# One paced list for the modulation columns of a conditioned two-layer trunk, with loads three columns ahead

## The chip, the cores and the metric

The kernel runs on one core of a Trainium2 chip. The metric is the device time of one execution in microseconds; lower is better.

## The reference

A trunk of two layers over 512 tokens of width 1024 in float32. A conditioning vector `c` gives every layer its shifts, scales and gates:

```
cs  = silu(c)
mod = cs @ mod_w[l] + mod_b[l]         # 6 x 1024 values: sh1, sc1, gt1, sh2, sc2, gt2
h = rmsnorm(x)*g*(1 + sc1) + sh1
x = x + gt1 * mixer(h)                 # layer 0: gated DeltaNet with 8 heads, layer 1: differential attention
h = rmsnorm(x)*g*(1 + sc2) + sh2
x = x + gt2 * (relu(h @ w1)**2 @ w2)   # w1 1024 x 4096, w2 4096 x 1024
```

Layer 1 also reads a shared `kv` projection, modulated by `cs @ kv_mod_w`. A last rmsnorm ends it. In all 96 + 16 = 112 columns of 128 modulation values are computed, each from a 128 x 1024 block of weights.

## The kernel before

**Data.** Activations lie with the features on the partitions: `x` is eight tiles of 128 x 512 (features x tokens). Every large product is done in three matmuls (`three`, L275 to L278): weights and activations are split in a high and a low part, and high by high, high by low and low by high are summed. `weights` (L264) loads a pair of weight tiles (`raw`, three buffers, 512 KB mostly), copies the high part on ACT (`wh`, L269), and subtracts for the low part (`wl`, L260), on DVE for the heads, gates and `w_out`, on POOL for the MLP. It then calls `mod_next` (L272).

**Order of the stages in layer 0.** The program first norms and modulates `x`, using columns 0 to 15; those are loaded at once and do not change here. Then come eight heads: `proj_head` (projection) and the generator `gdn` (three parts: the triangular inverse, the scan over four chunks, the output), each head's later parts overlapping the next head's projection. The gate projections follow, then head 7's last part, then `close_block` for `a_w_out` (L728): the first half of its columns in one piece (`proj_T`, then `add_resid` at L334), the second half in two token halves of 256 (`proj_halves`), where `done` adds the residual (L322), norms (L236 to L242) and modulates (L252 to L255). The block opens the second set of PSUM banks only when the first `add_resid` has read the old ones. MLP 0 follows: four quarters of `w1` (q0 to q3), with `relu` and square at L744 to L749, then `w2` in two column pieces of 16 row tiles, each ended by `add_resid` from the same four `j` banks; then the same again for the second half of the hidden width.

**The modulation columns.** A column is one load of 128 x 1024 float32 (512 KB, L181, on SP's queue) into a tile `mw`, and one instruction on DVE (L182, "a dot") that multiplies by `cs` and sums into one column of `raw_mod`. `mod_bias` and `mod_gsc` then finish groups of eight. Columns 16 to 23 are issued after head 3 and 24 to 31 after head 5, eight at a time (L704 to L708). Columns 32 to 111 stand in a list; each call of `weights` adds `rate` to a counter and takes that many columns off (L185): 1 in `w_out`, 1.2 in MLP 0. `mw` has two buffers, so a load waits for the dot two columns earlier. In columns 32, 33, 40 and 41 a one-element copy on POOL (L180, `gate_on`) makes the load wait for the output of head 4, or for a modulated tile of MLP 0's input.

**What sets the order.** Each engine runs its instructions in one fixed order, and so does SP with its loads. That order is not the order of the code: a scheduler in the framework places each engine's instructions ahead of time, so an edit of the list moves instructions of other lines too. The rows of the two orders below are its result.

Of the kernel before, what the change touches and what calls it, by code (L numbers as in the profile page):

```python
# [10 lines left out]
F32 = mybir.dt.float32  # L11
# [19 lines left out]
RAW = 3  # L31
MB = 8
NE = (0, 1, 2, 1, 2, 0, 1, 0)
CV = 9
GH = 4
GX = 7

# [3 lines left out]
C_GMIX = C_KVMODB + 16  # L41
# [43 lines left out]
def trunk_kernel(ctx: ExitStack, tc: tile.TileContext, a, outT):  # L85
# [32 lines left out]
    def big(pool, tag, bufs, dt=F32):  # L118
        return pool.tile([P, S], dt, tag=tag, name=nm(tag), bufs=bufs)
# [53 lines left out]

    queue, rate, due, gate_on = [], [0], [0], {}

    def mod_col(c, after=None, pool=None, bufs=2):
        src = a["mod_wT"][c * P:(c + 1) * P, :] if c < 96 else a["kv_mod_wT"][(c - 96) * P:(c - 95) * P, :]
        w = (pool or c_pool).tile([P, D], F32, tag="mw", name=nm("mw"), bufs=bufs)
        if after is not None:
            G.tensor_copy(w[0:1, 0:1], after[0:1, 0:1])  # L180
        nc.sync.dma_start(w, src)  # L181
        V.scalar_tensor_tensor(out=w, in0=w, scalar=1.0, in1=cs, op0=ALU.mult, op1=ALU.mult,  # L182
                               accum_out=raw_mod[:, c:c + 1])

    def mod_next(n):  # L185

        due[0] += n
        while due[0] >= 1 and queue:
            due[0] -= 1
            c, then = queue.pop(0)  # L190
            mod_col(c, gate_on.pop(c, None))
            for f in then:
                f()

    def mod_bias(lo, hi):
        V.tensor_tensor(out=mod[:, lo:hi], in0=raw_mod[:, lo:hi], in1=cols[:, lo:hi], op=ALU.add)
# [183 lines left out]
    for k0 in range(0, KT, 2):  # L380
        ws = []
        for h in range(2):
            k = k0 + h
            mod_col(SH1 + k, None, m_pool, MB)
            mod_col(SC1 + k, None, m_pool, MB)
            both = slice(k, k + 9, 8)
            V.tensor_tensor(out=mod[:, both], in0=raw_mod[:, both], in1=cols[:, both], op=ALU.add)
            mod_gsc(k, SC1 + k, C_GMIX + k, 1)
            modulate(k, xs, rb, 0, SH1, hh, hl, FULL)
            ws.append(head_weights(h, k0))  # L390
# [93 lines left out]
    def gdn(h):  # L484
# [27 lines left out]
        pk = natural(kT[h])  # L512
        kn = big(g_pool, "kn", 4)
        A.activation(kn, pk, AF.Copy)
# [8 lines left out]

        bq = [big(g_pool, "bq", 8) for _ in range(2)]
        for n in range(2):
# [161 lines left out]
    def gate(h0, n):  # L687
        ps = proj_T(cols_of(w_in, 3072 + P * h0, P * n), KT, hh, hl, ntile=n)
        for j in range(n):
# [3 lines left out]
            if oT[h] is not None:  # L693
                V.tensor_tensor(out=oT[h], in0=sz[h], in1=oT[h], op=ALU.mult)

    heads = []
    for h in range(H):
        proj_head(h)
        heads.append(gdn(h))
        next(heads[h])  # L700
        next(heads[h])
        if h:
            next(heads[h - 1], None)
        if h in (3, 5):  # L704
            c0 = 16 if h == 3 else 24
            for c in range(c0, c0 + 8):
                mod_col(c)
            mod_bias(c0, c0 + 8)  # L708
    for i in range(0, H, 2):
        gate(i, 2)  # L710
    next(heads[H - 1], None)
    for c in range(32, 112):
        queue.append((c, []))
    for c, j, sc, g_ in ((40, 8, SC2, C_GMLP), (64, 16, 48 + SC1, C_GMIX + 8), (88, 24, 48 + SC2, C_GMLP + 8), (112, 32, 104, C_GKV)):
        queue[c - 33][1].append(lambda j=j, sc=sc, g_=g_: mod_gsc(j, sc, g_))
    for c in range(40, 113, 8):
        queue[c - 33][1].insert(0, lambda c=c: mod_bias(c - 8, c))
    rate[0] = 1
    gate_on.update({32: oT[GH], 33: oT[GH]})
    g_st.close()  # L720
# [47 lines left out]

    rate[0] = 1.2
    gate_on.update({c: uh[GX].bitcast(F32) for c in (40, 41)})  # L770
    mlp(0, uh, ul, after0)
# [219 lines left out]
```

## Time and profile before

| | |
|---|---|
| median of 3 runs | 1413.43 us (1410.11 to 1415.57) |
| profiled execution | 1411.8 us |
| its span in the trace | 1410.0 us |
| PE busy | 1313.9 us, 93% |
| DVE busy | 800.0 us, 57% |
| ACT, POOL busy | 510.0 us, 481.9 us |
| mean granted TensorE clock | 0.977 |

The span is what the trace covers; the profiled execution's own time is 1.8 us longer, and lies 1.6 us under the median. PE is busy nearly throughout, so a change of the time has to be read from the 96 us in which it is not, and from what may be added to them. A full-width matmul (128 x 512) begins every 0.227 us when PE does not wait; a pair of weight tiles for four output tiles is 24 of these, 5.45 us.

### The profile page before, as it was taken

What the parts mean: (1) busy time and instruction counts of PE and PEld (TensorE: products, weight loads), DVE (VectorE), ACT (ScalarE), POOL (GpSimd) and SP (SyncE); (2) the same over time, 40 slices, a digit from 0 to 9 for tenths busy, and PEclk for the clock granted to TensorE, in tenths of its full rate; (3) what the DMA queues carried; (4) which work ended last, traced back from release to release, by engine and by line L of the source; (5) the groups of instructions that cost most, each with busy time, mean ns of one, the idle gap of its engine ahead of it and who ended that gap; (6) DMA issues with size and microseconds to landing.
All of it is one profiled execution on the core that took longest, in us unless ns stands there. A gap on an engine that the chain in (4) does not pass through costs nothing. (4 is left out here: it accounts for less than half of the span.)

```text
span 1410.0 us, 19521 instructions
## 1 busy us (share of the span) xinstructions
PE 1313.9 (93%) x7432; PEld 1111.3 (79%) x7432; DVE 800.0 (57%) x1688; ACT 510.0 (36%) x853; POOL 481.9 (34%) x285
## 2 busy tenths in 40 slices
PE   4888799899999999499999999999999999999997
PEld 3666687777789887388888998888798888888896
DVE  6999889788767877657311377777652110021113
ACT  3384234442424332122432244444434331243321
POOL 3324213221105454244544213232234444444441
PEclk9999699999999999799999999999999999999999
DMA  9542162112555777776322233221122232223221
GB/s 313 182 116 59 31 174 64 50 34 67 166 185 180 264 228 254 253 256 237 118 92 96 82 104 100 80 64 65 60 76 105 90 105 90 105 90 105 91 75 60
DMA packets 113214, 174.99 MB, mean 124 GB/s; under 512 B 16384, under 2 KB 56992, under 8 KB 113120
## 3 DMA queue, kind: packets, MB, share of 16 engines
q1 hardware_dynamic: 112416, 172.92, 37.6%
q8 instruction: 58, 0.95, 0.3%
q10 hardware_dynamic: 704, 0.83, 0.2%
q14 instruction: 36, 0.29, 0.1%
HBM read 170.04 MB, written 2.62 MB: 122 GB/s over the span
## 5 line engine op out<-in xcount | busy, mean ns | idle before, releaser
L260 POOL TENSOR_TENSOR wl<-raw,wh 128x1024 fp32r<-128x1024 f32 (+1 forms) x137 | 340.7, 2491 | 407.4 <-ACT wh L269 401.8
L269 ACT ACTIVATE wh<-raw 128x1024 fp32r<-128x1024 f32 (+2 forms) x217 | 215.4, 996 | 495.4 <-PE pj L277 279.8
L276 PE MATMUL pj<-h,wh 128*128 128x512 f32 (+1 forms) x816 | 290.8, 360 | 19.1 <-ACT h L254 7.6
L278 PE MATMUL pj<-h,wl 128*128 128x512 f32 (+1 forms) x816 | 290.4, 358 | 0.0
L277 PE MATMUL pj<-h,wh 128*128 128x512 f32 (+1 forms) x816 | 289.8, 355 | 0.0
L182 DVE SCALAR_TENSOR_TENSOR mw<-mw,cs 128x1024 f32<-128x1024 f32 x112 | 181.8, 1626 | 67.8 <-DMA mw<-in_mod_wT_dram 54.1
L276 PE MATMUL pj<-u,wh 128*128 128x512 f32 (+1 forms) x512 | 172.9, 338 | 17.7 <-DVE x L322 17.7
L276 PEld LDWEIGHTS pj<-h,wh 128*128 128x128 f32 x816 | 155.9, 192 | 40.2 <-ACT h L254 10.1
L278 PE MATMUL pj<-u,wl 128*128 128x512 f32 (+1 forms) x512 | 173.1, 338 | 2.7 <-POOL wl L260 2.7
L277 PE MATMUL pj<-u,wh 128*128 128x512 f32 (+1 forms) x512 | 172.9, 338 | 0.0
L277 PEld LDWEIGHTS pj<-h,wh 128*128 128x128 f32 x816 | 156.3, 192 | 17.9 <-DVE h L255 0.3
L278 PEld LDWEIGHTS pj<-h,wl 128*128 128x128 f32 x816 | 156.2, 192 | 18.1
L276 PEld LDWEIGHTS pj<-u,wh 128*128 128x128 f32 x512 | 97.7, 191 | 28.2 <-issue 18.1
L322 DVE SCALAR_TENSOR_TENSOR x<-pj,mod,x 128x256 f32<-128x256 f32 (+1 forms) x53 | 30.2, 585 | 156.3 <-PE pj L278 156.3
L278 PEld LDWEIGHTS pj<-u,wl 128*128 128x128 f32 x512 | 97.6, 191 | 13.6 <-POOL wl L260 3.5
L277 PEld LDWEIGHTS pj<-u,wh 128*128 128x128 f32 x512 | 97.6, 191 | 10.3
L260 DVE TENSOR_TENSOR wl<-raw,wh 128x1024 fp32r<-128x1024 f32 (+2 forms) x80 | 85.4, 1069 | 18.8 <-ACT wh L269 18.3
L745 DVE SCALAR_TENSOR_TENSOR pj<-pj,r 128x512 f32<-128x512 f32 x32 | 21.8, 693 | 71.7 <-ACT r L744 71.5
L745 DVE SCALAR_TENSOR_TENSOR pn<-pn,r 128x512 f32<-128x512 f32 x16 | 11.1, 693 | 74.8 <-ACT r L744 74.8
L276 PE MATMUL pn<-h,wh 128*128 128x512 f32 x128 | 49.8, 389 | 0.0
L277 PE MATMUL pn<-h,wh 128*128 128x512 f32 x128 | 49.8, 389 | 0.0
L278 PE MATMUL pn<-h,wl 128*128 128x512 f32 x128 | 49.8, 389 | 0.0
(297 smaller groups left out, 2366.5 us busy)
## 6 DMA issues: line engine op xcount, KB each, us to landing
raw<-in_mlp_w_dram SPq DMA_DIRECT2D x128, 512.0 KB, 3.6
mw<-in_mod_wT_dram SPq DMA_DIRECT2D x96, 512.0 KB, 4.4
raw<-in_a_w_in_dram SPq DMA_DIRECT2D x96, 128.0 KB, 2.5
mw<-in_kv_mod_wT_dram SPq DMA_DIRECT2D x16, 512.0 KB, 4.2
raw<-in_kv_w_dram SPq DMA_DIRECT2D x16, 512.0 KB, 3.3
x<-in_xT_dram SPq DMA_DIRECT2D x16, 256.0 KB, 5.6
raw<-in_a_w_in_dram SPq DMA_DIRECT2D x16, 256.0 KB, 2.7
raw<-in_a_w_out_dram SPq DMA_DIRECT2D x8, 512.0 KB, 4.8
```

The lines of the kernel that those rows point to most:

```text
L182: V.scalar_tensor_tensor(out=w, in0=w, scalar=1.0, in1=cs, op0=ALU.mult, op1=ALU.mult, accum_out=raw_mod[:, c:c + 1])
L260: (V if n else G).tensor_tensor(out=out, in0=x, in1=hi.bitcast(F32), op=ALU.subtract)
L269: A.activation(wh, raw, AF.Copy)
L276: T.matmul(ps, lhsT=wh, rhs=xh, start=first, stop=False, skip_group_check=skip)
L277: T.matmul(ps, lhsT=wh, rhs=xl, start=False, stop=False, skip_group_check=skip)
L278: T.matmul(ps, lhsT=wl, rhs=xh, start=False, stop=last, skip_group_check=skip)
L322: V.scalar_tensor_tensor(out=x[d][:, sl], in0=ps[j][:, sl], scalar=mod[:, gt + d:gt + d + 1], in1=x[d][:, sl], op0=ALU.mult, op1=ALU.add)
L745: V.scalar_tensor_tensor(out=ps[j], in0=ps[j], scalar=0.0, in1=r, op0=ALU.max, op1=ALU.mult)
```

## The change

All columns from 16 to 111 go in one list from the start of the heads. Each call of `weights` counts 0.5 in the heads and gates, 1 in `w_out` and 1.1 in MLP 0. A column is split in `mod_load` and `mod_dot`: a ring holds up to three loaded columns, and a load is issued when the dot three columns ahead of it is; `mw` gets four buffers. The copies that held loads back (`gate_on`) go, as do the two groups of eight after heads 3 and 5. Two tags of the heads' pool lose buffers (`kn` 4 to 3, `bq` 8 to 6).

```diff
--- before.py
+++ after.py
@@ -30,10 +30,9 @@
 SUB = 16
 RAW = 3
 MB = 8
+AHEAD = 3
 NE = (0, 1, 2, 1, 2, 0, 1, 0)
 CV = 9
-GH = 4
-GX = 7
 
 
 C_MODB = 0
@@ -171,26 +170,37 @@
     raw_mod = cp.tile([P, 112], F32, name="raw_mod")
     gsc = cp.tile([P, 40], F32, name="gsc")
 
-    queue, rate, due, gate_on = [], [0], [0], {}
-
-    def mod_col(c, after=None, pool=None, bufs=2):
+    queue, rate, due, ring = [], [0], [0], []
+
+    def mod_load(c, pool=None, bufs=AHEAD + 1):
         src = a["mod_wT"][c * P:(c + 1) * P, :] if c < 96 else a["kv_mod_wT"][(c - 96) * P:(c - 95) * P, :]
         w = (pool or c_pool).tile([P, D], F32, tag="mw", name=nm("mw"), bufs=bufs)
-        if after is not None:
-            G.tensor_copy(w[0:1, 0:1], after[0:1, 0:1])
         nc.sync.dma_start(w, src)
+        return w
+
+    def mod_dot(c, w):
         V.scalar_tensor_tensor(out=w, in0=w, scalar=1.0, in1=cs, op0=ALU.mult, op1=ALU.mult,
                                accum_out=raw_mod[:, c:c + 1])
 
+    def mod_col(c, pool, bufs):
+        mod_dot(c, mod_load(c, pool, bufs))
+
+    def mod_fill():
+        while queue and len(ring) < AHEAD:
+            c, then = queue.pop(0)
+            ring.append((c, mod_load(c), then))
+
     def mod_next(n):
 
         due[0] += n
-        while due[0] >= 1 and queue:
+        while due[0] >= 1 and (ring or queue):
             due[0] -= 1
-            c, then = queue.pop(0)
-            mod_col(c, gate_on.pop(c, None))
+            mod_fill()
+            c, w, then = ring.pop(0)
+            mod_dot(c, w)
             for f in then:
                 f()
+            mod_fill()
 
     def mod_bias(lo, hi):
         V.tensor_tensor(out=mod[:, lo:hi], in0=raw_mod[:, lo:hi], in1=cols[:, lo:hi], op=ALU.add)
@@ -381,8 +391,8 @@
         ws = []
         for h in range(2):
             k = k0 + h
-            mod_col(SH1 + k, None, m_pool, MB)
-            mod_col(SC1 + k, None, m_pool, MB)
+            mod_col(SH1 + k, m_pool, MB)
+            mod_col(SC1 + k, m_pool, MB)
             both = slice(k, k + 9, 8)
             V.tensor_tensor(out=mod[:, both], in0=raw_mod[:, both], in1=cols[:, both], op=ALU.add)
             mod_gsc(k, SC1 + k, C_GMIX + k, 1)
@@ -510,7 +520,7 @@
         G.tensor_tensor(out=v3(ex), in0=v3(ex), in1=m4(m_le), op=ALU.mult)
 
         pk = natural(kT[h])
-        kn = big(g_pool, "kn", 4)
+        kn = big(g_pool, "kn", 3)
         A.activation(kn, pk, AF.Copy)
         ssk = sumsq(kn, "sqk")
         V.tensor_scalar(out=ssk, in0=ssk, scalar1=EPS, scalar2=None, op0=ALU.add)
@@ -521,7 +531,7 @@
         V.tensor_tensor(out=sj, in0=sj, in1=beta[:, :, h], op=ALU.mult)
 
 
-        bq = [big(g_pool, "bq", 8) for _ in range(2)]
+        bq = [big(g_pool, "bq", 6) for _ in range(2)]
         for n in range(2):
             ps = bank("a")
             for c in (2 * n, 2 * n + 1):
@@ -693,6 +703,13 @@
             if oT[h] is not None:
                 V.tensor_tensor(out=oT[h], in0=sz[h], in1=oT[h], op=ALU.mult)
 
+    for c in range(16, 112):
+        queue.append((c, []))
+    for c, j, sc, g_ in ((40, 8, SC2, C_GMLP), (64, 16, 48 + SC1, C_GMIX + 8), (88, 24, 48 + SC2, C_GMLP + 8), (112, 32, 104, C_GKV)):
+        queue[c - 17][1].append(lambda j=j, sc=sc, g_=g_: mod_gsc(j, sc, g_))
+    for c in range(24, 113, 8):
+        queue[c - 17][1].insert(0, lambda c=c: mod_bias(c - 8, c))
+    rate[0] = 0.5
     heads = []
     for h in range(H):
         proj_head(h)
@@ -701,22 +718,11 @@
         next(heads[h])
         if h:
             next(heads[h - 1], None)
-        if h in (3, 5):
-            c0 = 16 if h == 3 else 24
-            for c in range(c0, c0 + 8):
-                mod_col(c)
-            mod_bias(c0, c0 + 8)
+    rate[0] = 0.5
     for i in range(0, H, 2):
         gate(i, 2)
     next(heads[H - 1], None)
-    for c in range(32, 112):
-        queue.append((c, []))
-    for c, j, sc, g_ in ((40, 8, SC2, C_GMLP), (64, 16, 48 + SC1, C_GMIX + 8), (88, 24, 48 + SC2, C_GMLP + 8), (112, 32, 104, C_GKV)):
-        queue[c - 33][1].append(lambda j=j, sc=sc, g_=g_: mod_gsc(j, sc, g_))
-    for c in range(40, 113, 8):
-        queue[c - 33][1].insert(0, lambda c=c: mod_bias(c - 8, c))
     rate[0] = 1
-    gate_on.update({32: oT[GH], 33: oT[GH]})
     g_st.close()
     np_, np_st = open_pool("np", bufs=2)
     ogh, ogl = h_tiles()
@@ -766,8 +772,7 @@
         for k in range(KT):
             modulate(k, xs, rb, 16, 48 + SH1, qh, ql, sl)
 
-    rate[0] = 1.2
-    gate_on.update({c: uh[GX].bitcast(F32) for c in (40, 41)})
+    rate[0] = 1.1
     mlp(0, uh, ul, after0)
     rate[0] = 0
     c_st.close()
```

The two orders, at three places. In these rows `mw` is a column's tile, `wl<-raw,wh` the low part of a weight pair, `h<-x,h` the low part of a head's output; numbers behind names count tiles. Lines of the changed kernel are 10 higher there (L332 is L322 of before, L270 is L260); the dot is at L182 in both, the load at L181 before and L178 now.

DVE, at the end of head 7, ahead of the first `add_resid` of `w_out` (`x<-pj,mod,x`). Before:

```order
L260 TENSOR_TENSOR h_3717<-x_3691,h_3716 128x512
L260 TENSOR_TENSOR wl_3915<-raw_3911,wh_3913 128x1024
L182 SCALAR_TENSOR_TENSOR mw_3917,raw_mod<-mw_3917,cs 128x1024
L260 TENSOR_TENSOR wl_3924<-raw_3920,wh_3922 128x1024
L182 SCALAR_TENSOR_TENSOR mw_3926,raw_mod<-mw_3926,cs 128x1024
L182 SCALAR_TENSOR_TENSOR mw_3935,raw_mod<-mw_3935,cs 128x1024
L260 TENSOR_TENSOR wl_3933<-raw_3929,wh_3931 128x1024
L322 SCALAR_TENSOR_TENSOR x_3872<-pj_3734,mod,x_3872 128x512
L322 SCALAR_TENSOR_TENSOR x_3874<-pj_3735,mod,x_3874 128x512
L182 SCALAR_TENSOR_TENSOR mw_3944,raw_mod<-mw_3944,cs 128x1024
L228 TENSOR_TENSOR acc_3889<-acc_3889,nsq_3892 128x512
L322 SCALAR_TENSOR_TENSOR x_3876<-pj_3736,mod,x_3876 128x512
```

Now:

```order
L206 TENSOR_TENSOR mod<-raw_mod,cols 128x8
L182 SCALAR_TENSOR_TENSOR mw_4757,raw_mod<-mw_4757,cs 128x1024
L686 TENSOR_TENSOR ro_3705<-ro_3705,rq_3290 128x4
L182 SCALAR_TENSOR_TENSOR mw_4760,raw_mod<-mw_4760,cs 128x1024
L182 SCALAR_TENSOR_TENSOR mw_4794,raw_mod<-mw_4794,cs 128x1024
L692 SCALAR_TENSOR_TENSOR x_3709<-pr_3710,cols,cv_3696 128x512
L182 SCALAR_TENSOR_TENSOR mw_4827,raw_mod<-mw_4827,cs 128x1024
L270 TENSOR_TENSOR h_3735<-x_3709,h_3734 128x512
L182 SCALAR_TENSOR_TENSOR mw_4892,raw_mod<-mw_4892,cs 128x1024
L182 SCALAR_TENSOR_TENSOR mw_4925,raw_mod<-mw_4925,cs 128x1024
L332 SCALAR_TENSOR_TENSOR x_3890<-pj_3752,mod,x_3890 128x512
L332 SCALAR_TENSOR_TENSOR x_3892<-pj_3753,mod,x_3892 128x512
```

Before, the dots of columns 0 to 38 stand ahead of the first `add_resid`; now those of 0 to 61 do, 23 more. Between head 7's T matrix and the low part of its output (`h`) stand 21 dots now, columns 40 to 60, of which the rows above show the last five.

SP's queue, at the first weight loads of MLP 0. Before:

```order
L143 DMA x_3886<-in_xT_dram 128x512
L181 DMA mw_3926<-in_mod_wT_dram 128x1024
L267 DMA raw_3929<-in_a_w_out_dram 128x2x512
L181 DMA mw_3935<-in_mod_wT_dram 128x1024
L267 DMA raw_3938<-in_a_w_out_dram 128x2x512
L181 DMA mw_3944<-in_mod_wT_dram 128x1024
L267 DMA raw_4276<-in_mlp_w_dram 128x2x512
L267 DMA raw_4286<-in_mlp_w_dram 128x2x512
L267 DMA raw_4296<-in_mlp_w_dram 128x2x512
L267 DMA raw_4305<-in_mlp_w_dram 128x2x512
L267 DMA raw_4538<-in_mlp_w_dram 128x2x512
```

Now:

```order
L277 DMA raw_4310<-in_mlp_w_dram 128x2x512
L178 DMA mw_4991<-in_mod_wT_dram 128x1024
L178 DMA mw_5056<-in_mod_wT_dram 128x1024
L178 DMA mw_5089<-in_mod_wT_dram 128x1024
L178 DMA mw_5124<-in_mod_wT_dram 128x1024
L178 DMA mw_5157<-in_mod_wT_dram 128x1024
L178 DMA mw_5160<-in_mod_wT_dram 128x1024
L178 DMA mw_5193<-in_mod_wT_dram 128x1024
L178 DMA mw_5226<-in_mod_wT_dram 128x1024
L178 DMA mw_5259<-in_mod_wT_dram 128x1024
L277 DMA raw_4319<-in_mlp_w_dram 128x2x512
L277 DMA raw_4553<-in_mlp_w_dram 128x2x512
```

Before, five weight loads of MLP 0 follow each other behind column 39. Now nine column loads (63 to 71) stand between the third and the fourth, and the last reload of `x` stands right behind the load of column 61 (36 before).

DVE, ahead of `w2`'s first `add_resid` in MLP 0. Before:

```order
L182 SCALAR_TENSOR_TENSOR mw_5670,raw_mod<-mw_5670,cs 128x1024
L182 SCALAR_TENSOR_TENSOR mw_5703,raw_mod<-mw_5703,cs 128x1024
L182 SCALAR_TENSOR_TENSOR mw_5706,raw_mod<-mw_5706,cs 128x1024
L182 SCALAR_TENSOR_TENSOR mw_5771,raw_mod<-mw_5771,cs 128x1024
L182 SCALAR_TENSOR_TENSOR mw_5804,raw_mod<-mw_5804,cs 128x1024
L182 SCALAR_TENSOR_TENSOR mw_5837,raw_mod<-mw_5837,cs 128x1024
L322 SCALAR_TENSOR_TENSOR x_3872<-pj_5037,mod,x_3872 128x512
L322 SCALAR_TENSOR_TENSOR x_3874<-pj_5038,mod,x_3874 128x512
L182 SCALAR_TENSOR_TENSOR mw_5870,raw_mod<-mw_5870,cs 128x1024
L322 SCALAR_TENSOR_TENSOR x_3876<-pj_5039,mod,x_3876 128x512
L322 SCALAR_TENSOR_TENSOR x_3878<-pj_5040,mod,x_3878 128x512
```

Now:

```order
L755 TENSOR_TENSOR u_5036<-pm_4883,u_5034 128x512
L751 SCALAR_TENSOR_TENSOR pm_4884<-pm_4884,r_5038 128x512
L182 SCALAR_TENSOR_TENSOR mw_6730,raw_mod<-mw_6730,cs 128x1024
L755 TENSOR_TENSOR u_5043<-pm_4884,u_5041 128x512
L206 TENSOR_TENSOR mod<-raw_mod,cols 128x8
L209 SCALAR_TENSOR_TENSOR gsc<-mod,cols 128x8
L332 SCALAR_TENSOR_TENSOR x_3890<-pj_5045,mod,x_3890 128x512
L332 SCALAR_TENSOR_TENSOR x_3892<-pj_5046,mod,x_3892 128x512
L332 SCALAR_TENSOR_TENSOR x_3894<-pj_5047,mod,x_3894 128x512
L332 SCALAR_TENSOR_TENSOR x_3896<-pj_5048,mod,x_3896 128x512
L332 SCALAR_TENSOR_TENSOR x_3898<-pj_5322,mod,x_3898 128x512
```

Before, columns up to 85 stand ahead of it, with the last six in a row; now all 112 do, the last dot two rows of the `relu` and two small sums ahead, and no dot follows.

## Rows read from the trace of the kernel before

**Rows 1.** The page's busy times: engine, busy us with its share of the span, instructions.

```profile
PE 1313.9 (93%) x7432; PEld 1111.3 (79%) x7432; DVE 800.0 (57%) x1688; ACT 510.0 (36%) x853; POOL 481.9 (34%) x285
```

**Rows 2.** The page's groups: line, engine and operation, what is written and read with shapes, count | busy us, mean ns of one | idle us of the engine just before them and what ended most of it.

```profile
L276 PE MATMUL pj<-u,wh 128*128 128x512 f32 (+1 forms) x512 | 172.9, 338 | 17.7 <-DVE x L322 17.7
L182 DVE SCALAR_TENSOR_TENSOR mw<-mw,cs 128x1024 f32<-128x1024 f32 x112 | 181.8, 1626 | 67.8 <-DMA mw<-in_mod_wT_dram 54.1
```

**Rows 3.** A table of stretches of the span (start and end in us, length; then busy us of PE, its weight loads, DVE, ACT and POOL, each with its instructions; the granted clock of TensorE as a share of its full level; the share of time that the DMA engines were busy; GB/s).

```profile
340.00:403.85 63.85, 62.12 (x359) 49.67 (x358) 45.70 (x100) 24.20 (x41) 5.59 (x6) 1.00 0.58 188
403.85:436.00 32.15, 29.86 (x235) 28.78 (x234) 18.89 (x43) 12.74 (x23) 9.20 (x5) 1.00 0.23 79
436.00:461.00 25.00, 24.55 (x193) 23.82 (x192) 19.90 (x36) 10.24 (x18) 11.91 (x8) 1.00 0.69 233
461.00:567.00 106.00, 103.32 (x454) 84.88 (x454) 81.85 (x104) 33.68 (x47) 51.00 (x19) 1.00 0.75 248
567.00:586.00 19.00, 3.17 (x14) 2.28 (x13) 11.46 (x14) 2.11 (x2) 5.78 (x3) 0.71 0.70 247
```

**Rows 4.** The same table, from a second set of stretches.

```profile
20.00:40.00 20.00, 15.41 (x59) 11.44 (x58) 18.41 (x21) 5.32 (x7) 10.97 (x5) 1.00 1.00 328
85.20:340.00 254.80, 228.44 (x1524) 184.63 (x1524) 224.16 (x664) 109.40 (x188) 71.90 (x58) 0.93 0.27 73
```

**Rows 5.** DVE in order of time, from head 7 to the second half of `w_out`: start us, duration us, line and operation, in brackets the idle us before it and what ended it.

```profile
349.37 0.68 DVE L568 TENSOR_TENSOR t<-tc,mask 128x512 f32<-128x512 f32 x1
...
391.26 0.68 DVE L260 TENSOR_TENSOR h<-x,h 128x512 fp32r<-128x512 f32 x1
401.38 1.23 DVE L182 SCALAR_TENSOR_TENSOR mw<-mw,cs 128x1024 f32<-128x1024 f32 x1 [1.75 <-DMA mw<-in_mod_wT_dram]
403.85 1.41 DVE L322 SCALAR_TENSOR_TENSOR x<-pj,mod,x 128x512 f32<-128x512 f32 x2
...
418.66 0.48 DVE L322 SCALAR_TENSOR_TENSOR x<-pj,mod,x 128x256 f32<-128x256 f32 x1 [7.17 <-PE pj L278]
```

**Rows 6.** PE in order of time, the same stretch and columns.

```profile
387.91 0.66 PE L488 MATMUL pr<-mask,o 128*128 128x128 f32 x4 [1.71 <-POOL o L677]
...
403.63 0.39 PE L276 MATMUL pj<-h,wh 128*128 128x512 f32 x1
403.86 0.39 PE L277 MATMUL pj<-h,wh 128*128 128x512 f32 x1
...
409.03 0.36 PE L276 MATMUL pj<-h,wh 128*128 128x256 f32 x1 [1.84 <-ACT nsq L227]
```

**Rows 7.** What DVE waited for between 340 and 404 us: us in total, times, longest.

```profile
DVE wl L260 <- ACT wh L269: 5.8, 6, 3.0
DVE mw L182 <- DMA mw<-in_mod_wT_dram: 2.3, 2, 1.8
DVE ro L676 <- POOL ro L675: 2.0, 2, 1.1
DVE st L665 <- ACT o L661: 1.8, 2, 1.2
```

**Rows 8.** DVE in order of time, from the modulation of the second token half to the first `relu` of MLP 0.

```profile
435.03 0.88 DVE L255 SCALAR_TENSOR_TENSOR h<-pm,mod,h 128x256 fp32r<-128x256 f32 x2
438.73 0.16 DVE L239 TENSOR_SCALAR rs<-pn 128x2 f32<-128x2 f32 x1 [0.76 <-PE pn L236]
440.94 1.23 DVE L182 SCALAR_TENSOR_TENSOR mw<-mw,cs 128x1024 f32<-128x1024 f32 x1 [2.05 <-DMA mw<-in_mod_wT_dram]
...
458.86 2.17 DVE L182 SCALAR_TENSOR_TENSOR mw<-mw,cs 128x1024 f32<-128x1024 f32 x1 [1.17 <-DMA mw<-in_mod_wT_dram]
460.95 1.29 DVE L745 SCALAR_TENSOR_TENSOR pj<-pj,r 128x512 f32<-128x512 f32 x2
```

**Rows 9.** PE in order of time, at the change from the first to the second half of `w2`'s columns in MLP 0.

```profile
569.78 0.39 PE L278 MATMUL pj<-u,wl 128*128 128x512 f32 x1
587.92 0.76 PE L276 MATMUL pj<-u,wh 128*128 128x512 f32 x1 [17.75 <-DVE x L322]
588.48 0.63 PE L277 MATMUL pj<-u,wh 128*128 128x512 f32 x1
...
591.89 0.43 PE L276 MATMUL pj<-u,wh 128*128 128x512 f32 x1
```

**Rows 10.** DVE in order of time, just ahead of the first of those matmuls.

```profile
582.59 1.22 DVE L182 SCALAR_TENSOR_TENSOR mw<-mw,cs 128x1024 f32<-128x1024 f32 x1 [0.71 <-DMA mw<-in_mod_wT_dram]
...
585.87 1.23 DVE L182 SCALAR_TENSOR_TENSOR mw<-mw,cs 128x1024 f32<-128x1024 f32 x1 [2.05 <-DMA mw<-in_mod_wT_dram]
...
587.02 1.41 DVE L322 SCALAR_TENSOR_TENSOR x<-pj,mod,x 128x512 f32<-128x512 f32 x2
```

**Rows 11.** The dot products (L182) that began between 85 and 230 us, those between 60 and 404 us and those between 436 and 586 us: count, shortest, median and longest in ns, first and last start in us.

```profile
L182 DVE SCALAR_TENSOR_TENSOR mw<-mw,cs x15: 1203/1206/1219, 88.7 to 224.0; 128x1024 f32<-128x1024 f32 x15
L182 DVE SCALAR_TENSOR_TENSOR mw<-mw,cs x25: 1203/1211/2864, 58.8 to 401.4; 128x1024 f32<-128x1024 f32 x25
L182 DVE SCALAR_TENSOR_TENSOR mw<-mw,cs x46: 1210/1368/3410, 440.9 to 585.9; 128x1024 f32<-128x1024 f32 x46
```

**Rows 12.** The DMA queue of SP over the whole span: what an issuing line waited for, us in total, times, longest.

```profile
SPq L181 <- DVE mw L182: 165.8, 76, 10.2
```

## The prediction

> **What bounds the kernel now.** I read the busy times first: PE works 1313.9 of 1410.0 us [rows 1], so only its 96 idle us can be won, and anything that makes PE wait longer is lost whole. The costliest groups come next. The dots take DVE 181.8 us and had it waiting 67.8 us, mostly for their loads; and one group of PE, the first matmuls of `w2`, waited 17.7 us for `add_resid` on DVE [rows 2]. So the columns reach the end of the kernel by one way only: DVE runs in a fixed order, and where dots stand ahead of something that PE needs, PE pays.
>
> The table of stretches shows where that is. From 340 to 567 us PE is busy 219.9 of 227 us, and from 567 to 586 us 3.2 of 19 [rows 3]. PE in order of time shows that hole: the last matmul of `w2`'s first half begins at 569.78 us, the next at 587.92, after 17.75 us of waiting for L322 [rows 9]. DVE in order of time shows why: `add_resid` begins at 587.02 us, when the last of a row of dots is through, and these had waited 0.7 to 2.05 us each for loads [rows 10]. The loads themselves wait for dots: SP's queue stood 165.8 us for a dot to free a buffer [rows 12]. That is what two buffers do, and what a ring of three loads with four buffers can take away.
>
> The other place is the end of the heads. `add_resid` of `w_out` begins at 403.85 us with DVE busy right up to it [rows 5], and PE does not wait for it: its own last matmuls run past 403.63 us, and its longest wait behind is 1.84 us at 409.03 [rows 6]. The two engines arrive together; there is no slack on DVE.
>
> **The change, term by term.**
>
> *Ahead of `w_out`'s `add_resid`: +20 us.* The new order puts 23 more dots ahead of it. A dot takes 1.21 us here (median), 1.23 at the end [rows 5, 11]: 23 by 1.22 is 28.1 us. DVE is busy 45.70 of 63.85 us between 340 and 403.85 us [rows 3], so 18.15 us are free. Of these 5.8 us wait for ACT's high parts and 2.3 us for a column's load [rows 7]; both shrink when DVE runs late and loads run ahead. 8.1 us filled leave 20. The rest of the idle time is in steps of 1 or 2 us of head 7's chain (output norm, scan) [rows 7]: a dot put there covers the wait, but the next step starts when the dot ends, so I count no gain. Bounds: filling all 18.15 us leaves +10; filling also some of the 30.6 us that DVE is free between 85 and 340 us [rows 4], since 8 of the 23 dots stand ahead of head 7's T matrix, leaves 0. The upper end comes from the loads. The stretch moves 188 GB/s for 63.85 us [rows 3], 12.0 MB; 23 columns of 0.524 MB add 12.1. At the 328 GB/s of the start [rows 4] 24.1 MB take 73 us, +10; at the 248 of the MLP [rows 3] 97 us, +33. I take 20, from DVE, whose rows are those of the stretch itself. PE has nothing to put there: the block's second half needs the banks that `add_resid` reads, and in PE's new order three of the four weight pairs of the first half already stand among head 7's steps. Only half a pair, 12 matmuls of 0.23 us [rows 6] or 2.7 us, is left behind head 7's last transposes, where now 16 us of PE's work lie between these (387.91 us) [rows 6] and `add_resid`.
>
> *Norm and modulation of the two token halves: +7 us.* For the first half, five dots (66 to 70) now stand between the residual and the last modulated tile, where there was none: 6.1 us. PE covers with the second half's matmuls, but before the change these end as the modulation ends (435.03 us) [rows 8]; I take +4, from 0 (all covered) to +8 (two waits for loads of 2.05 us [rows 8] each, on top). Dots 62 to 65 stand ahead of the second residual, where DVE waited 7.17 us for PE [rows 5], and cost nothing. For the second half nine dots (71 to 79) stand in place of seven, four of them ahead of the norm at 438.73 us, where there was none [rows 8]. Two more are 2.4 us; +3, from 0 to +6.
>
> *The hole at `w2`: -17.75 us.* All 112 dots now stand ahead of its `add_resid`, but they have begun earlier: between the two `add_resid` there are 50 dots against 47. Three more at 1.37 us [rows 11] are 4 us, and DVE is idle 42.5 of the 163.15 us between 403.85 and 567 us [rows 3]. The loads fit as well: 2.5, 5.8 and 26.3 MB in the three stretches [rows 3], 1.6 MB more is 222 GB/s over the whole, less than the 248 that the third reached. So the hole goes, nearly whole; bounds -18 and, if the last three dots are still 3.3 us apart as at 582.59 and 585.87 [rows 10], -8. Late next is PE itself.
>
> *The clock: 0.* After the hole PE ran at the lower of its levels: matmuls from 588.48 to 591.89 us begin 0.43 us apart against 0.227 [rows 9], 1.8 us in all, with the granted clock at 0.71 in that stretch [rows 3]. This goes with the hole; a wait of 20 us at `w_out` should bring the same back.
>
> *The rest: 0.* The groups of eight were no bursts in the trace: 15 of their 16 dots lie between 88.7 and 224.0 us [rows 11]. Six dots at head 0 in place of two cost up to 5 us there and are given back by the heads behind; -6 to +6. The four POOL copies held only loads; the dot behind the last two waited 2.05 us [rows 8], the most they can give. Fewer `kn` and `bq` buffers make a tile wait for its reader of three heads ago, long done; if not, 2.0 us as the chain's waits [rows 7] a head.
>
> Sum: 20 + 7 - 17.75 = +9. The profiled execution took 1411.8 us, 1.6 less than the median; 1420.8 there, 1422.4 on the median, rounded to **1422.5**.
>
> **The rivals.** About 0.5%, 7 us, is what a measurement of this kernel can tell from no change.
>
> *Faster: the dots drop into the gaps.* If head 7's chain loses nothing to the dots between its steps, `add_resid` is late by 0 to 10 us, the first half's modulation is covered, and the hole goes: -18 to -8, about 1400. For it: 18.15 us idle on DVE in that stretch, and loads three ahead remove the 2 us waits. Against it: DVE has no gap right ahead of 403.85 us, and the chain's gaps are each about one dot long. It decides at a delay of 11 us at `w_out`: below it the change wins. Chance 0.24. The Trainium skill ("Trainium Kernel Development and Optimization", Best Practices) says to double-buffer for performance, so that DMA overlaps compute; by that rule alone a deeper ring can only win, and the time would be this rival's. The 165.8 us that SP's queue waited for dots [rows 12] bear the rule out for the MLP; it says nothing on what the earlier dots push back on DVE.
>
> *Level.* The delay is 13 us rather than 20 and the modulation costs 4: -1, 1412, within 0.5%. For it: half of the chain's gaps filled. Chance 0.20.
>
> *Much slower: the loads bind.* SP's queue now has nine columns between the third and fourth weight load of MLP 0, and `x` behind column 61. If the tail runs at 248 GB/s, `add_resid` is 33 us late; the nine columns take 19 us, and the time from the second residual to the end of the first half's modulation (418.66 to 435.03 us) [rows 5, 8] covers 16 of them, so the weights come 3 us late: 33 + 7 + 3 - 18 = +25, 1438. For it: MLP 0 never moved more than 248 [rows 3]. Against it: 328 were seen [rows 4]. Chance 0.16.
>
> That the change does not do what it says is excluded in part: SP's rows show the loads well ahead of the dots. But the pace of 0.5 and 1 is not kept, since the order puts 21 dots into head 7's tail.
>
> **How the numbers follow.** The likeliest case has 0.40, its own range 1415 to 1432. With the rivals: faster 0.24, same 0.20, slower 0.56. The ends are 1393 (0 at `w_out`, all of the hole) and 1452 (+33, +14, -8); leaving out a tenth at either side gives 1399 to 1443.
>
> **What would show it.** Right: `add_resid` of `w_out` begins near 424 us in a row of dots, PE waits some 20 us for it there, the wait of 17.75 us at `w2` is gone, and PE's lower clock is found at about 425 us. Wrong: a wait of under 11 us at `w_out` (the gaps took the dots), a wait at `w2` that stays, or PE waiting for weight loads at the start of MLP 0.

## The result, and the profile after

The changed kernel takes 1397.85 us (median of 4 runs, 1396.40 to 1401.83) against 1413.21 us (median of 4, 1410.11 to 1415.57): a ratio of 0.9897, 95% interval 0.9869 to 0.9925. It is faster by 1.0%, where 1422.5 us and slower were forecast; the lower end of the range was 1399. The profiled execution has a span of 1396.3 us, 13.7 us less.

The page's groups of after (columns as in [rows 2]):

```profile
L182 DVE SCALAR_TENSOR_TENSOR mw<-mw,cs 128x1024 f32<-128x1024 f32 x112 | 170.4, 1532 | 6.3 <-DMA mw<-in_mod_wT_dram 4.4
L286 PE MATMUL pj<-u,wh 128*128 128x512 f32 (+1 forms) x512 | 172.0, 336 | 0.0
```
DVE's idle time ahead of the dots falls from 67.8 us [rows 2] to 6.3, the part that waited for loads from 54.1 to 4.4, and `w2`'s first matmuls wait for nothing. The stretches (columns as in [rows 3]):

```profile
85.20:340.00 254.80, 234.48 (x1573) 188.56 (x1573) 230.18 (x674) 113.98 (x197) 76.00 (x58) 0.96 0.31 85
340.00:400.00 60.00, 51.95 (x307) 42.09 (x306) 56.24 (x125) 20.81 (x34) 3.93 (x3) 0.94 0.83 276
400.00:440.00 40.00, 33.57 (x219) 30.67 (x218) 33.53 (x59) 9.90 (x17) 10.69 (x6) 0.88 0.78 263
470.00:570.00 100.00, 100.00 (x443) 82.81 (x442) 77.57 (x98) 34.53 (x48) 50.91 (x20) 1.00 0.73 254
570.00:610.00 40.00, 40.00 (x179) 33.10 (x178) 3.00 (x4) 7.43 (x7) 17.45 (x8) 1.00 0.28 93
```
From 85 to 340 us PE works 234.48 us instead of 228.44 [rows 4], at a mean clock of 0.96 instead of 0.93. From 340 to 440 us it loses: 85.5 us busy where it had 95.5, with a clock of 0.94 and 0.88 where both stretches had 1.00. From 470 to 610 us it is never idle. DVE in order of time, from head 7's T matrix to `add_resid` of `w_out` (columns as in [rows 5]):

```profile
363.36 0.68 DVE L578 TENSOR_TENSOR t<-tc,mask 128x512 f32<-128x512 f32 x1
...
408.55 1.23 DVE L182 SCALAR_TENSOR_TENSOR mw<-mw,cs 128x1024 f32<-128x1024 f32 x1 [0.37 <-DMA mw<-in_mod_wT_dram]
...
409.70 2.06 DVE L332 SCALAR_TENSOR_TENSOR x<-pj,mod,x 128x512 f32<-128x512 f32 x3
```
And PE there:

```profile
403.60 0.66 PE L498 MATMUL pr<-mask,o 128*128 128x128 f32 x4 [0.27 <-POOL o L687]
...
407.96 0.63 PE L288 MATMUL pj<-h,wl 128*128 128x512 f32 x1
408.38 0.63 PE L287 MATMUL pj<-h,wh 128*128 128x512 f32 x1
...
412.48 0.38 PE L286 MATMUL pj<-h,wh 128*128 128x256 f32 x1 [1.86 <-DVE x L332]
```
`add_resid` begins at 409.70 us right behind a dot, 5.85 us later than before [rows 5], not 20. (From the T matrix to `h` the trace has 20 dots, columns 40 to 59; 60 and 61 follow `h`.) PE arrives hardly sooner: its matmuls from 407.96 us still begin 0.42 us apart, the lower clock, and it waits 1.86 us for DVE. At `w2`, PE:

```profile
577.79 0.39 PE L288 MATMUL pj<-u,wl 128*128 128x512 f32 x1
578.01 0.39 PE L286 MATMUL pj<-u,wh 128*128 128x512 f32 x1
```
and DVE:

```profile
574.13 0.75 DVE L332 SCALAR_TENSOR_TENSOR x<-pj,mod,x 128x512 f32<-128x512 f32 x1 [23.67 <-PE pj L288]
```
The last matmul of the first half and the first of the second are 0.22 us apart, where 18.14 us lay between [rows 9]; DVE now waits 23.67 us for PE.

So, against the kernel before: 5.85 us late at `w_out`, 8.0 late at the end of `w2`'s first half (577.79 against 569.78 us), 9.9 early behind it (578.01 against 587.92), 11.9 early with the 2.0 us of lower clock gone that followed the hole (the first `add_resid` of MLP 0's second half of the hidden width at 748.21 against 760.10 us), and 13.7 at the end. These two rows are DVE's at 760.10 and 748.21 us, before and after:

```profile
760.10 0.75 DVE L322 SCALAR_TENSOR_TENSOR x<-pn,mod,x 128x512 f32<-128x512 f32 x1 [35.38 <-PE pn L278]
748.21 0.75 DVE L332 SCALAR_TENSOR_TENSOR x<-pn,mod,x 128x512 f32<-128x512 f32 x1 [35.39 <-PE pn L288]
```

### The profile page after: what moved, and what is told of

It reads as the page before. It is cut to its first block, busy times and chain, and to the rows that moved or that the text cites. A ratio compares the mean times of both kernels' runs of the same rounds, so it can differ in the third digit from the quotient of the medians.

```text
span 1396.3 us, 19499 instructions
## 1 busy us (share of the span) xinstructions
PE 1315.4 (94%) x7432; PEld 1112.7 (80%) x7432; DVE 780.9 (56%) x1688; ACT 510.8 (37%) x853; POOL 483.5 (35%) x281
## 5 line engine op out<-in xcount | busy, mean ns | idle before, releaser
L270 POOL TENSOR_TENSOR wl<-raw,wh 128x1024 fp32r<-128x1024 f32 (+1 forms) x137 | 332.2, 2426 | 414.7 <-ACT wh L279 414.7
L182 DVE SCALAR_TENSOR_TENSOR mw<-mw,cs 128x1024 f32<-128x1024 f32 x112 | 170.4, 1532 | 6.3 <-DMA mw<-in_mod_wT_dram 4.4
L332 DVE SCALAR_TENSOR_TENSOR x<-pj,mod,x 128x256 f32<-128x256 f32 (+1 forms) x53 | 30.5, 585 | 214.8 <-PE pj L288 214.8
L270 DVE TENSOR_TENSOR wl<-raw,wh 128x1024 fp32r<-128x1024 f32 (+2 forms) x80 | 83.0, 1039 | 13.2 <-ACT wh L279 13.0
```

Of the source, the lines that this page charges most:

```text
L270: (V if n else G).tensor_tensor(out=out, in0=x, in1=hi.bitcast(F32), op=ALU.subtract)
L332: V.scalar_tensor_tensor(out=x[d][:, sl], in0=ps[j][:, sl], scalar=mod[:, gt + d:gt + d + 1], in1=x[d][:, sl], op0=ALU.mult, op1=ALU.add)
```

## The experiments

Theory A: PE pays at two places on DVE, at `w_out` and at `w2`; the gain is the hole at `w2`, less what earlier dots cost. Theory B: the gain is the ring's, through waits for loads. Theory C: the heads, without the groups of eight. All ran beside the kernel before; ratios are to it, with 95% intervals. The diffs are excerpts, with remarks put behind `#`; `...` stands for lines left out.

One trace is one execution. Three pairs have the same instructions in the same order on every engine up to 440 us, yet their first `add_resid` differ: by 1.6 us (before and 1), 3.0 (2 and 5) and 2.5 (7 and 8). So single starts in the table tell nothing under 3 us. The time from head 7's T matrix to `add_resid` repeats better: 36.92 and 36.93 us in 2 and 5.

| kernel | first `add_resid`, us | columns ahead of it | ahead of `w2`'s | wait at `w2`, us | median, us | ratio |
|---|---|---|---|---|---|---|
| before | 403.85 | 39 | 86 | 17.75 | 1411.3 to 1413.2 | 1 |
| changed | 409.70 | 62 | 112 | 0 | 1397.85 | 0.9897 |
| 1 | 405.41 | 39 | 72 | 0 | 1394.96 | 0.9876 (0.9858 to 0.9893) |
| 2 | 401.34 | 40 | 94 | 13.70 | 1400.03 | 0.9918 (0.9900 to 0.9937) |
| 3 | 404.62 | 49 | 102 | 19.55 | 1411.28 | 0.9996 (0.9984 to 1.0009) |
| 4 | 410.68 | 41 | 109 | 11.26 | 1414.04 | 1.0024 (1.0014 to 1.0034) |
| 5 | 398.38 | 40 | 72 | 0 | 1384.28 | 0.9798 (0.9781 to 0.9816) |
| 6 | 409.18 | 58 | 112 | 0 | 1398.89 | 0.9898 (0.9874 to 0.9922) |
| 7 | 397.46 | 39 | 86 | 19.9 | 1406.33 | 0.9962 (0.9946 to 0.9978) |
| 8 | 394.97 | 39 | 72 | 0 | 1385.12 | 0.9814 (0.9776 to 0.9852) |
| 9 | 407.99 | 61 | 112 | 0 | 1402.79 | 0.9933 (0.9916 to 0.9949) |
| 10 | 406.11 | 69 | 112 | 0 | 1393.96 | 0.9874 (0.9851 to 0.9897) |
| 11 | 403.67 | 48 | 102 | 13.6 | 1403.39 | 0.9934 (0.9913 to 0.9955) |

**1. The hole alone.**

```diff
+    queue.extend(full[:40])                               # columns 32 to 71
...
     add_resid(xs, 4 * q, proj_T(cols_of(w2, 512 * q), 16, uh, ul), gt)
+    if q == layer == 0:
+        due[0] = 0
+        queue.extend(full[40:])                           # columns 72 to 111
+        gate_on.update({c: xs[3] for c in (72, 73)})
```

> The kernel before, with one edit: columns 72 to 111 are put on the list only when the first add_resid of w2 in MLP 0 is written, and the loads of columns 72 and 73 wait for it, so 72 columns stand ahead of it instead of 86. Two buffers, groups after heads 3 and 5, and the order up to w_out stay. Theory A (the gain of the change is the hole of 17.75 us at w2 and its 1.8 us of lower clock, less what the earlier dots cost at w_out): the wait at w2 is gone, 1413 - 17.75 - 1.8 = about 1394, between 1391 and 1398. Theory B (the gain is the removed waits for loads, by the deeper ring): still two buffers, so 1410 to 1414. Theory C (the gain is in the heads, where the groups of eight no longer stand): 1412 to 1414.

DVE in order of time, at `w_out` and at `w2`:

```profile
405.41 1.42 DVE L322 SCALAR_TENSOR_TENSOR x<-pj,mod,x 128x512 f32<-128x512 f32 x2
...
565.60 0.75 DVE L322 SCALAR_TENSOR_TENSOR x<-pj,mod,x 128x512 f32<-128x512 f32 x1 [20.30 <-PE pj L278]
```
`add_resid` of `w2` now waits 20.30 us for PE, no longer the other way round, and 17 us are gone, with two buffers and no ring. Theory A holds; B and C do not explain this. The moved dots are not free: behind the hole, up to 745 us, PE waits 2.9 us for low parts from POOL, where the changed kernel waits for nothing from 578 to 748 us.

**2. Columns 40 up held until MLP 0.**

```diff
+    after = gate_on.pop(c, None)                          # in mod_load
+    if after is not None:
+        G.tensor_copy(w[0:1, 0:1], after[0:1, 0:1])
...
+    queue.extend(full[:24])                               # columns 16 to 39
...
-    rate[0] = 1.1
+    queue.extend(full[24:])                               # columns 40 to 111
+    rate[0], due[0] = 1.2, 0
+    gate_on.update({c: uh[7].bitcast(F32) for c in range(40, 44)})
```

> The changed kernel with columns 40 to 111 put on the list only at MLP 0 (rate 1.2), the loads of 40 to 43 waiting for its last modulated input tile: 40 columns stand ahead of w_out's first add_resid instead of 62, and 94 ahead of w2's. Theory A: the first add_resid is at about 404 us instead of 409.7 and the modulation 2 us faster, together -8; at w2 54 dots and 24 weight loads, 41 MB, have to pass in 166 us, 247 GB/s, which the ring can just do: a wait of 0 to 8 us there, so 1390 to 1398. Theory B (loads ahead are what counts): as the changed kernel, 1396 to 1400. My prediction's price of 20 us for the 23 dots would give 1397.9 - 27 = 1371 with no wait at w2.

DVE at head 7's T matrix and at `w_out`, and then PE at `w2`:

```profile
364.42 0.68 DVE L581 TENSOR_TENSOR t<-tc,mask 128x512 f32<-128x512 f32 x1
...
401.34 0.75 DVE L335 SCALAR_TENSOR_TENSOR x<-pj,mod,x 128x512 f32<-128x512 f32 x1 [2.23 <-PE pj L291]
```
```profile
578.96 0.76 PE L289 MATMUL pj<-u,wh 128*128 128x512 f32 x1 [13.70 <-DVE x L335]
```
With 22 columns fewer ahead, `add_resid` begins 8.4 us earlier than in the changed kernel (11.3 in 5, the same code up to there), and waits 2.23 us for PE. But held dots begin at 437.9 us, and the hole is back with 13.70 us. The wait was bounded at 8: a miss in size. The time, 1400.03 us, is outside theory A's range and at the end of B's, so it does not decide; that `add_resid` moved and the hole came back does. The changed kernel's early dots buy the hole's end.

**3 and 4. The pace without the ring, the ring without the pace.**

```diff
-            mod_fill()                                    # 3: load and dot together
-            c, w, then = ring.pop(0)
-            mod_dot(c, w)
+            c, then = queue.pop(0)
+            mod_col(c, None, 2)
```

```diff
-            c, then = queue.pop(0)                        # 4: in the kernel before; mw 4 (was 2), kn 3 (was 4), bq 6 (was 8) buffers
-            mod_col(c, gate_on.pop(c, None))
+            mod_fill()
+            c, w, then = ring.pop(0)
+            mod_dot(c, w)
```

> The changed kernel without the ring: each load is issued with its dot and mw has two buffers, as before; one list and its rates stay. 49 columns stand ahead of w_out's first add_resid and 102 ahead of w2's. Theory A: the place at w2 decides. 53 dots at the 3.2 us that two buffers gave before are 170 us in 166 us of PE work: a wait of 4 to 12 us at w2, and 2 to 3 us at w_out, so 1399 to 1408. Theory B (the ring is the gain): 1410 to 1416. Theory C (heads): 1398 to 1404.

> The kernel before with the ring alone: the list from column 32 on goes through a ring of three with four buffers (kn 3, bq 6 to make room); the groups of eight after heads 3 and 5, the four POOL copies and the rates stay. 41 columns stand ahead of w_out's first add_resid, 109 ahead of w2's. Theory A: 68 dots and 24 weight loads are 48 MB between the two, 166 us at the 290 GB/s that the changed kernel reached on average there at its best: a wait of 0 to 20 us at w2, so 1395 to 1414, and the dots' waits for loads shrink without that mattering. Theory B (the ring is the gain): 1395 to 1399. Theory C: 1410 to 1414.

PE at `w2`, in 3 and in 4:

```profile
589.79 0.76 PE L284 MATMUL pj<-u,wh 128*128 128x512 f32 x1 [19.55 <-DVE x L330]
```
```profile
594.04 0.77 PE L291 MATMUL pj<-u,wh 128*128 128x512 f32 x1 [11.26 <-DVE x L337]
```
Neither is faster. In 3 the hole is larger than forecast, 19.55 us, with 102 columns ahead of it and two buffers; the time, 1411.28 us, missed theory A's range and lies in B's. In 4 the hole is 11.26 us, and `add_resid` of `w_out` is 6.8 us later, at 410.68 us, in a trace of the slowest of its ten runs; theory B, which expected the whole gain in 4, falls. Room for the ring took buffers from `kn` and `bq` in 4, as in the changed kernel; what that costs by itself was not tested. Ring and pace each leave the hole; of the two, only both together close it.

**5. Held at both places.**

```diff
-    queue.extend(full[24:])                               # 2
+    queue.extend(full[24:56])                             # columns 40 to 71
...
+    if q == layer == 0:                                   # behind w2's first add_resid, as in 1
+        due[0] = 0
+        queue.extend(full[56:])
+        gate_on.update({c: xs[3] for c in (72, 73, 74, 75)})
```

> The second experiment (columns 40 up held until MLP 0's input) with columns 72 to 111 also held behind w2's first add_resid: 40 columns ahead of w_out's first add_resid, 72 ahead of w2's. Theory A (two places on DVE, each paid by PE): add_resid of w_out at 401 us as with the second experiment, and its 13.7 us at w2 with 1.8 us of lower clock go: 1400 - 15.5 = about 1384.5, between 1382 and 1388, 10 to 15 us under the changed kernel. If DVE's load of dots after w2 makes a new wait in the second half of MLP 0, 1388 to 1395. Theory C (the heads decide): as the second experiment, about 1400.

DVE at head 7's T matrix and at both places:

```profile
361.45 0.68 DVE L581 TENSOR_TENSOR t<-tc,mask 128x512 f32<-128x512 f32 x1
...
398.38 0.75 DVE L335 SCALAR_TENSOR_TENSOR x<-pj,mod,x 128x512 f32<-128x512 f32 x1 [2.23 <-PE pj L291]
...
556.77 0.75 DVE L335 SCALAR_TENSOR_TENSOR x<-pj,mod,x 128x512 f32<-128x512 f32 x1 [25.36 <-PE pj L291]
```
Both gains add up: 1384.28 us, with 8 the fastest, 1.0% under the changed kernel.

**6. Light dots.** The dots of columns 40 to 61 go over 128 of their 1024 elements: this kernel leaves out 7/8 of these sums. The loads stay whole.

```diff
+        n = 128 if 40 <= c < 62 else D
-        V.scalar_tensor_tensor(out=w, in0=w, ...)
+        V.scalar_tensor_tensor(out=w[:, 0:n], in0=w[:, 0:n], ...)
```

> The changed kernel with the dots of columns 40 to 61 over 128 of their 1024 elements (7/8 of these sums are left out); their loads stay whole. 58 columns stand ahead of w_out's first add_resid, 18 of them light. Theory A (DVE's work delays it): 18 us of DVE work less; add_resid at 401 to 404 us instead of 409.7, and the run about 6 us faster than the changed kernel, 1390 to 1394. Rival (the loads delay it, 291 GB/s between head 7's T matrix and add_resid): at 408 to 411 us, 1396 to 1400.

DVE, and then the stretches of 5 us (columns as in [rows 3]):

```profile
374.68 0.29 DVE L183 SCALAR_TENSOR_TENSOR mw<-mw,cs 128x128 f32<-128x128 f32 x1 [3.02 <-DMA mw<-in_mod_wT_dram]
...
409.18 2.07 DVE L333 SCALAR_TENSOR_TENSOR x<-pj,mod,x 128x512 f32<-128x512 f32 x3 [0.79 <-PE pj L289]
```
```profile
375.00:380.00 5.00, 4.65 (x21) 3.51 (x22) 2.02 (x8) 1.06 (x1) 0.00 (x0) 0.50 0.59 196
380.00:385.00 5.00, 5.00 (x16) 4.20 (x15) 2.06 (x7) 0.00 (x0) 0.00 (x0) 0.50 0.53 139
```
`add_resid` does not move, as the rival said. But it does not settle the matter: a dot waited 3.02 us for its load inside head 7's chain, and from 375 to 385 us PE ran at half clock, where the changed kernel had 1.00; the trace is of the slowest of four runs, 5 us above their median. It may be that one delay took the place of another.

**7. The pace of the heads alone.**

```diff
-        if h in (3, 5):                                   # in the kernel before
...
+    for c in range(16, 32):
+        queue.append((c, []))
+    rate[0] = 0.5
```

> The kernel before with one edit: columns 16 to 31 go through the list at 0.5 a call in the heads, in place of the two groups of eight. Two buffers, copies on POOL, w_out and MLP 0 as before; 39 columns ahead of w_out's first add_resid, 86 ahead of w2's. Theory A: the heads are worth some 2 to 6 us (PE had done 6 us more by 360 us in the changed kernel), the 17.75 us at w2 stay: 1406 to 1412. Theory C (the heads carry the gain): 1396 to 1401. Rival (the groups cost nothing): 1411 to 1414.

Stretches of the heads, in the kernel before and here:

```profile
140.00:160.00 20.00, 17.06 (x144) 14.83 (x144) 16.87 (x55) 6.89 (x12) 2.30 (x2) 0.84 0.11 31
160.00:180.00 20.00, 14.87 (x54) 11.77 (x54) 16.91 (x50) 5.55 (x12) 8.16 (x7) 0.53 0.25 71
260.00:280.00 20.00, 15.12 (x121) 12.71 (x120) 15.69 (x36) 9.05 (x15) 2.66 (x3) 0.83 0.16 43
```
```profile
140.00:160.00 20.00, 20.00 (x169) 16.77 (x169) 16.71 (x55) 6.29 (x13) 2.86 (x3) 1.00 0.10 25
160.00:180.00 20.00, 16.41 (x87) 12.22 (x87) 19.29 (x54) 9.46 (x18) 7.29 (x7) 1.00 0.52 135
260.00:280.00 20.00, 20.00 (x155) 16.43 (x155) 17.94 (x61) 3.35 (x8) 4.88 (x3) 1.00 0.27 70
```
and DVE at `w_out`:

```profile
397.46 0.75 DVE L322 SCALAR_TENSOR_TENSOR x<-pj,mod,x 128x512 f32<-128x512 f32 x1
```
6.4 us are won by `w_out`, and stay. The clock shows where: in these three stretches it stood at 0.84, 0.53 and 0.83 before, and at 1.00 here; over 85.2 to 349.37 us its mean goes from 0.93 to 0.97. The time, from nine runs, is 6.3 us under the kernel before (3.1 to 7.6 by the interval). Theory A's size was right; C, that the heads carry it all, was not.

**8. The two edits of 1 and 7 together.**

```diff
-        if h in (3, 5):                                   # in the kernel before: 7
...
+    rate[0] = 0.5
...
+        gate_on.update({c: xs[3] for c in (72, 73)})      # and 1
```

> The kernel before with the two edits of the first and the seventh experiment together: columns 16 to 31 paced at 0.5 in the heads, columns 72 to 111 held behind w2's first add_resid. No ring, two buffers. Theory A (heads and hole are separate gains, and the ring is none): 1412.5 - 6.3 - 17 = about 1389, between 1386 and 1392. Theory B (the ring is part of what the fifth experiment won): 1395 or more. If the heads' gain is lost in the rest, 1394 to 1396.

1385.12 us, from 1381.74 to 1393.65: the median is 4 us under the sum of the two gains, about 1389, which the interval covers (1381 to 1392 us); it is as fast as 5 within the intervals, and with two buffers. The ring is not needed for it.

**9, 10, 11. What is left of the delay at `w_out`.**

```diff
-            xs.extend(load_x())                           # 9
+            xs.extend(load_x(nc.gpsimd))
```

```diff
+        n = 128 if 40 <= c < 62 else D                    # 10, with the dots of 6
-        nc.sync.dma_start(w, src)
+        nc.sync.dma_start(w[:, 0:n], src[:, 0:n])
```

```diff
+    gate_on.update({c: uh[7].bitcast(F32) for c in range(48, 52)})   # 11, in the changed kernel
```

> The changed kernel with the reload of x in w_out issued on POOL's queue instead of SP's, where it stands behind the load of column 61. 61 columns ahead of w_out's first add_resid. Theory A1 (what is left of the delay at w_out is the reload of x behind the columns' loads): add_resid at 403 to 407 us instead of 409.7, 1392 to 1396. Theory A2 (it is PE's own order around head 7 and its lower clock, which the sixth experiment left in place): add_resid at 408 to 411, 1396 to 1400.

> The changed kernel with columns 40 to 61 cut to 128 of their 1024 elements in load and dot alike (7/8 of these sums are left out); 69 columns ahead of w_out's first add_resid, 22 of them cut. In the sixth experiment the loads had stayed whole, and DVE waited 3.0 us for one of them in head 7's chain. Theory A (the columns' work, dots and loads together, lengthens head 7's chain from 33 to 41 us): from T to the last transposes 31 to 35 us, add_resid at 400 to 405 us, 1388 to 1394. Theory A2 (PE's order around head 7 lengthens it): 40 us as before, add_resid at 408 to 411, 1396 to 1400.

> The changed kernel with the loads of columns 48 to 51 (where still to come at that point) waiting for MLP 0's last modulated input tile: 48 columns ahead of w_out's first add_resid, 102 ahead of w2's; between 40 (second experiment: add_resid at 401 us, 13.7 us of waiting at w2) and 62 (changed kernel: 409.7 and none). Theory A (each dot moved ahead of w_out costs there and is won at w2): add_resid at 402 to 406 us, 54 dots between the two places as in the second experiment, so the wait at w2 is again 8 to 15 us: 1398 to 1404. If filling head 7's gaps with eight columns is free and relieves w2 in full, 1390 to 1395.

DVE of 9, then of 10, and then of 11, at `add_resid`, with head 7's T matrix for the last two:

```profile
407.99 0.75 DVE L332 SCALAR_TENSOR_TENSOR x<-pj,mod,x 128x512 f32<-128x512 f32 x1 [0.95 <-DMA x<-in_xT_dram]
409.62 0.75 DVE L332 SCALAR_TENSOR_TENSOR x<-pj,mod,x 128x512 f32<-128x512 f32 x1 [0.88 <-DMA x<-in_xT_dram]
```
```profile
363.11 0.68 DVE L580 TENSOR_TENSOR t<-tc,mask 128x512 f32<-128x512 f32 x1
...
406.11 2.46 DVE L334 SCALAR_TENSOR_TENSOR x<-pj,mod,x 128x512 f32<-128x512 f32 x3 [0.79 <-PE pj L290]
```
```profile
363.32 0.68 DVE L581 TENSOR_TENSOR t<-tc,mask 128x512 f32<-128x512 f32 x1
...
403.67 1.41 DVE L335 SCALAR_TENSOR_TENSOR x<-pj,mod,x 128x512 f32<-128x512 f32 x2 [2.49 <-PE pj L291]
```
9 decides nothing: on POOL's queue `x` was issued at 402.3 us, behind POOL's own work for head 7, hardly sooner than at 403.1 in the changed kernel; `add_resid` now waits for `x` itself, and the time, 1402.79 us, is above both forecasts. 10, which leaves out 7/8 of the same sums and of their loads, begins `add_resid` 3.6 us earlier, between the two forecasts, and its time, 1393.96 us, is just inside theory A's range. From T it takes 43.00 us where the changed kernel takes 46.34: 3.3 us of the 9.4 that the latter has over 2, though seven full columns more stand ahead in 10.

11 says what a dot costs. From T to `add_resid` it takes 36.92 us in 2, with no dot between, 40.35 in 11 with 8 and 46.34 in the changed kernel with 22: 0.43 us a dot in both steps, with their loads, about a third of its 1.21 us. The hole stays at 13.6 us, with as many dots between the two `add_resid` as in 2.

## Why the prediction was wrong

**The hole at `w2`, -17.75: right.** It closed, and 1 shows it as a gain by itself. The clock behind it was worth another 2.0 us.

**Ahead of `w_out`, +20: this step failed**, in "I count no gain" for the gaps of head 7's chain. The stretch up to `add_resid` in the changed kernel (columns as in [rows 3]):

```profile
340.00:409.70 69.70, 59.63 (x328) 47.55 (x327) 64.67 (x138) 21.44 (x35) 7.11 (x4) 0.90 0.84 276
```
DVE is idle for 5.0 us there, against 18.15 before [rows 3]; from 85.2 to 340 us for 24.6, against 30.6 [rows 4]. So 13.1 and 6.0 us of idle time were filled, where the sum had 8.1 and 0. DVE's work in both stretches rose by 25.0 us, not 28.1; 19.1 of it went into idle time, and 5.85 is left. My own bound of 0 said that this could be; I took 20 because each gap is about one dot long. Measured by 2, 11 and the changed kernel, the 22 columns behind T cost 9.4 us, 0.43 each, where the sum had 0.87.

**The rest, 0 with -6 to +6: the second miss.** I took the groups of eight for harmless since their dots lay apart. 7 shows -6.4 us for pacing them, just outside my bounds. It is seen in the clock of the heads, which I had read for `w2` only. 9.4 less 6.4 is 3.0; the rest up to 5.85 is as much as two executions of the same code differ by, and whether the order, the ring or the fewer `kn` and `bq` buffers cost it is open.

**Norm and modulation, +7: mis-sized.** Between `w_out`'s first `add_resid` and the end of `w2`'s first half the changed kernel loses 2.2 us more (8.0 less 5.85). No experiment took it apart, and the kernel before and 1, the same code for half of that way, differ there by 2.1 (165.93 and 163.84 us).

**The clock, 0: half right.** It fell at `w_out`, as said (0.88 from 400 to 440 us), though not behind a wait of 20 us: PE had been busy 37.2 of the 46.34 us from T to `add_resid`, at 0.85. Its cost lies in the 5.85 and the 2.2.

The sum as it was: 5.85 + 2.2 - 17.9 - 2.0 = -11.9 us, and 1.8 more that appear behind 748.21 us, where the order differs too; these were not tested. The rival "faster" named the mechanism and the point from which it decides, 11 us at `w_out`; with 5.85 it won. The rule of the Trainium skill beside it ("Trainium Kernel Development and Optimization", Best Practices: double-buffer so that DMA overlaps compute) is not what decided: the ring without the pace, with the buffers it took from `kn` and `bq`, made the kernel 0.24% slower (0.14 to 0.34), and 8 gains 1.9% with two buffers.

**Open:** how the 9.4 us divide between the columns' work, the reload of `x` behind them and the order of PE's weight pairs around head 7 (10 gives at least 3.3 to the first; 6 and 9 did not separate the others), and what the buffers of `kn` and `bq` cost.

## What to carry to other kernels

Work added to an engine with gaps need not be paid at its full length, even where the gaps are as short as the work; here a third of it was paid. Bound it by the idle time of the whole stretch, and don't take the gaps between a chain's steps for lost without a measurement. Compare two executions of the same code before reading a difference of a few us from one trace of each. Where filler work stands ahead of something that the bounding engine needs, count it at every such place and move it behind; that gained more here than loading it earlier. Read the granted clock in stretches for the whole kernel, since short waits in a row can lower it as a long one does: before, it was 0.53 from 160 to 180 us, where no wait of PE was longer than 1.0 us, and 0.71 at the hole.

## What the runs showed of the hardware

A dot that meets POOL's subtraction waits for it. DVE and then POOL in 2:

```profile
567.67 1.22 DVE L185 SCALAR_TENSOR_TENSOR mw<-mw,cs 128x1024 f32<-128x1024 f32 x1
568.81 3.35 DVE L185 SCALAR_TENSOR_TENSOR mw<-mw,cs 128x1024 f32<-128x1024 f32 x1
```
```profile
568.46 2.63 POOL L273 TENSOR_TENSOR wl<-raw,wh 128x1024 fp32r<-128x1024 f32 x1 [3.34 <-ACT wh L282]
```
The first dot began before POOL and took 1.22 us. The second began while POOL worked and took 3.35: it ended at 572.16 us, 1.1 us after POOL's end at 571.09, about its own length. In 2, all 23 dots between 400 and 600 us that took over 1.5 us began while POOL subtracted and ended 1.1 us after it. POOL, which began during the first dot, took 2.63 us, and 2.34 the next time, at 573.58 us, when no dot was running as it began. The Trainium skill ("SBUF — State Buffer", Who interferes with whom) says that a DVE instruction with two SBUF inputs contends with a GpSimd instruction that reads SBUF, and calls the ports they share an exclusive lock; these rows agree, 3.35 us against 1.22. In 2 DVE was busy 94.4 of the 100 us from 470 to 570, 75.7 of them with 40 dots, which at 1.21 us would be 48. That these waits are why the ring did not make the held dots fast enough is likely, but no run took them away.
